# Turning the probabilities of seven head pairs on VectorE and through DRAM, in a one-core trunk layer

## The chip, the cores and the metric

The kernel runs on one core of a Trainium2 chip, in float32. The core has five engines with queues of their own: PE (TensorE, matrix products; PEld is its loading of the stationary operand), DVE (VectorE), ACT (ScalarE), POOL (GpSimd) and SP (SyncE, which here issues most DMAs). The metric is the device time of one execution in microseconds; the median of several runs counts.

## What is computed

One layer of a diffusion backbone for 128 context tokens and 256 latent tokens, width 2048: modulation by conditioning vectors, a combined projection to queries, keys, values and a Fourier group, attention, gates, an output projection, and a gated feed-forward part.

```python
sh1, sc1, g1, sh2, sc2, g2 = modulation(cond, w_mod_l, b_mod_l)
h = rms_norm(x, n1) * (1 + sc1) + sh1
q, k, v, u = project_in(h, w_in_l, qg_l, kg_l)
attn = attend(q, k, v)
x = x + g1 * token_mixing(h, attn, u, w_na_proj_l, w_fnet_proj_l, w_gate_l, w_o_l)
h2 = rms_norm(x, n2) * (1 + sc2) + sh2
x = x + g2 * swiglu(h2, w_gu_l, w_down_l)
```

Attention has 16 heads of 64. A context token attends to the 128 context tokens; a latent token to a window of the 256 latent tokens (a table of biases holds -1e30 outside it) and, in the same softmax, to 128 cached keys.

## The kernel before

**Products.** Every large weight comes in units of 256 rows by 512 columns (`load_unit`, issued on SP, four buffers). ACT makes a rounded high part `wh`, DVE the rest `wl` (`split`, L155 and L156), three buffers each; `unit` (L170, L171, L176) forms three products a block, 18 of 128x128 by 128x512 to a unit. `next_unit` is the heart of the order: it takes the `front` jobs one step further, splits the weights of the unit after this one, steps `front` and `behind` jobs, issues the load of a unit three further on, and hands the present one to PE. `mid_unit` steps `front` a third time in the middle of a unit.

**Order by pace.** All engines run their instructions in the order in which the program writes them, and that is written by generators: `Paced(gen, rate)` adds `rate` to what is due at each tick and runs a step (up to the next `yield`) for each whole one. `least` holds steps back until that many are due.

**Stages.** Opening (modulation, input projection; to about 320 us), gate stage (64 units of the gate projection, with the Fourier and attention work between them; to about 650), mixing stage (32 units), output stage (four column chunks of eight units; the first five units and the rest of the first chunk run with the row sums stopped), feed-forward part.

**Attention** is a generator in the gate stage, stepped three times a unit. `attention_pair` treats two heads: `PAIR` names what each of its 15 ticks does. `qk` turns queries and keys on PE, `s0` and `s1` form scores of the two latent token blocks (block 0 with the context tokens) and put them into `sc` (128 x 2 x 896), `m` takes maxima on DVE, `e` exponentials on ACT, `i` inverts the sums and scales `sc` on DVE (L1026). `t0` and `t1` (`keys_first`) transpose the 8 and 6 blocks of 128x128 on PE (L1039) into PSUM, from where ACT copies them (L1041) to `pt`; `pv` (`values`, L1056) multiplies by the values. `t1` and `pv` of a pair run in the next pair's ticks. `lq`, `lb`, `lv` issue the next loads.

**Row sums.** Four rows of the modulation (types 2, 4, 3, 5, in this order) are not formed on PE. `row_weights` loads 128x1024 blocks, and `mod_rows` adds them up on DVE (L361, L363; 32 such instructions for each half row, one a step). Then a chain of DMAs on POOL sums over the 128 partitions by halving (`s_sum`, L367 and L373) and adds the bias (L379, L380). `columns` reads a row back (`colr`, L391), has PE transpose it (L398) and DVE use it; type 4's columns come within type 3's sums, type 3's within type 5's, after the tenth of them. `RATES` gives the pace of these steps: at first, in the gate, mixing and output stages, and in the feed-forward part. In the output stage `rows_until` runs on until a row is done if it is not by then.

Of the kernel before, what the change touches and what calls it, by code (L numbers as in the profile page):

```python
# [13 lines left out]
F32 = mybir.dt.float32  # L14
F32R = mybir.dt.float32r
AF = mybir.ActivationFunctionType
# [3 lines left out]
P = 128  # L20
# [7 lines left out]
CTX = 128  # L28
LAT = 256
TOK = CTX + LAT  # L30
# [10 lines left out]
ORDER = [6, 7, 0, 1, 2, 3, 4, 5]  # L41
DUE = [-1.4, 0, 0, 0]
PREP = [1.75, 2.5, 1.8, 1.8]
PAIR = "t1 qk,,,,,lq,s0 s1 m0,e0,m1,i0 pv lb,e1,,i1 t0,,lv"

CHUNKS = [1.95, 1.95, 1.95, 1.6, 1.6, 1.2, 1.2, 1.7]
RATES = [1.5, 0.62, 1.1, 1.3, 0.452]
FF_PARTS = [8, 8, 8, 8, 12]  # L50


# [67 lines left out]
def trunk_kernel(ctx: ExitStack, tc: tile.TileContext, io: dict):  # L120
    nc = tc.nc
# [21 lines left out]
    dram = ctx.enter_context(tc.tile_pool(name="dram", bufs=1, space=DRAM))  # L143
# [6 lines left out]
    def nm(s):  # L150
        return f"{s}{next(ids)}"
# [133 lines left out]

    s_sum = dram.tile([P, 4 * CH], F32, tag="sum", name="s_sum")
    s_turn = dram.tile([P, 4, TOK], F32, tag="turn", name="s_turn")

    first = consts.tile([P, 96], F32, tag="first", name="first")
    conds, ng, bcol = (first[:, 32 * i : 32 * i + 32] for i in range(3))  # L290
# [16 lines left out]
    with ExitStack() as ph:  # L307
# [79 lines left out]
        def columns(ty):  # L387

            r = rpool.tile([32, P], F32, tag="colr", name=nm("colr"))
            for cnd in range(2):  # L390
                nc.gpsimd.dma_start(  # L391
                    r[16 * cnd : 16 * cnd + 16], s_row[ty][cnd].rearrange("o (k p) -> (o k) p", p=P)
                )
            yield
            yield
            yield
            o = rows_psum["tile"]()
            nc.tensor.transpose(o[:, 0:32], r, ident[:32, :32])  # L398
            ov = o[:, 0:32].rearrange("p (c k) -> p k c", c=2)
            yield  # L400
            if ty == 3:
                nc.vector.tensor_copy(msh[1], ov)
                return
            nc.vector.scalar_tensor_tensor(
                out=msc[1], in0=ov, scalar=1.0, in1=ng[:, 1].unsqueeze(2).to_broadcast([P, KT, 2]),
                op0=ALU.add, op1=ALU.mult,
            )
# [59 lines left out]
        with ExitStack() as pha:  # L467
# [37 lines left out]
            r1 = small.tile([P, NT], F32, tag="r1", bufs=1, name="r1")  # L505
# [50 lines left out]
            for t in range(NT):  # L556
                for cc in range(4):
                    turn(t, cc, acc_tile)
                    square(t, cc)
                    if t == 0 and cc == 2:  # L560
                        nc.scalar.activation(
                            out=csz[:, :, 0:2], in_=conds.rearrange("p (k c) -> p k c", c=2), func=AF.Silu
# [119 lines left out]
            for b, (i, t) in enumerate((i, t) for i in range(8) for t in range(NT)):  # L682
                ts = [slice(n * P, (n + 1) * P) for n in range(NT)]
                _, wH, wL = opened[i // 2]
                w, l = wH[:, i % 2], wL[:, i % 2]
                if b == 0:
                    po = [mm_tile() for _ in ts]
# [78 lines left out]
            for gi, (k0, n) in list(enumerate(GROUPS))[1:]:  # L766
# [5 lines left out]
                for rate, ci in zip(CHUNKS, ORDER):  # L772
                    if gi == len(GROUPS) - 1:
                        rows.rate = rate
                    po = [(mm_tile if gi < len(GROUPS) - 1 else acc_tile)() for _ in range(NT)]
# [130 lines left out]
        def attention():  # L906
            br = ph.enter_context(tc.tile_pool(name="branch", bufs=1))
            for i in range(8):
                aT[i] = br.tile([P, TOK], F32, tag=f"aT{i}", name=f"aT{i}")
            with ExitStack() as st:  # L910
                wk = st.enter_context(tc.tile_pool(name="awk", bufs=1))
                rest = {}
                for hp in range(8):
                    rest = yield from attention_pair(hp, wk, rest)
                rest["t1"]()
                for _ in range(5):
                    yield
                rest["pv"]()

        qks, vs, biases = [], [], []  # L920
        ending = [False]
# [10 lines left out]

        def load_v(hp):
            ci, co = hp // 4, (hp % 4) * P
            vp = ald.tile([P, 4, P], F32, tag="vp", bufs=2, name=nm("vp"))
            nc.sync.dma_start(vp[:, 0:3], s_qkvu[4 + ci][:, :, co : co + P])
            nc.sync.dma_start(vp[:, 3], cache_v[:, hp * P : (hp + 1) * P])
            return vp
# [7 lines left out]
        def attention_pair(hp, wk, rest):  # L946
            (_, (qp, kp)), (_, bp), (_, vp) = qks[0].take(), biases[0].take(), vs[0].take()
            t = {}

            sc = wk.tile([P, 2, 896], F32, tag="sc", name=nm("sc"))  # L950
# [70 lines left out]
            def inverses(qt):  # L1021
                sm = t["sm", qt]
                n = len(halves[qt])
                nc.vector.reciprocal(sm[:, :n], sm[:, :n])
                for i, (j, sl) in enumerate(halves[qt]):
                    nc.vector.tensor_scalar_mul(sc[:, j, sl], sc[:, j, sl], sm[:, i : i + 1])  # L1026

            def keys_first(qt):

                if not qt:  # L1030
                    t["pt"] = wk.tile([P, 16, P], F32, tag="pt", name=nm("pt"))
                blocks = [(j, qt * TOK + kc * P) for kc in range(3) for j in range(2)]
                if not qt:
                    blocks += [(j, 2 * TOK) for j in range(2)]
                for b0 in range(0, len(blocks), 4):
                    some = blocks[b0 : b0 + 4]
                    o = at_tile()
                    for i, (j, c0) in enumerate(some):
                        nc.tensor.transpose(o[:, i * P : (i + 1) * P], sc[:, j, c0 : c0 + P], ident)  # L1039
                    dst = slice(8 * qt + b0, 8 * qt + b0 + len(some))  # L1040
                    nc.scalar.copy(  # L1041
                        t["pt"][:, dst], o[:, : len(some) * P].rearrange("p (b q) -> p b q", q=P)
                    )

            def values():

                pt = t["pt"]
                po = at_tile()
                for k in range(4):
                    for j in range(2):  # L1050
                        s = slice(j * HD, (j + 1) * HD)
                        out, x = po[s, :CTX], pt[:, 6 + j]
                        if k:
                            out = po[s, CTX:TOK].rearrange("p (t q) -> p t q", t=2)
                            x = pt.rearrange("p (t b) q -> p t b q", t=2)[:, :, 2 * k - 2 + j]
                        nc.tensor.matmul(  # L1056
                            out, vp[:, k, s], x, start=k < 2, stop=k in (0, 3),
                            tile_position=(0, j * HD), skip_group_check=True,
                        )
                nc.scalar.copy(aT[hp], po[:, :TOK])  # L1060
# [2 lines left out]
                "qk": turned,  # L1063
                **{n: lambda of=of: of[0].more() for n, of in (("lq", qks), ("lb", biases), ("lv", vs))},
                **{f"{n}{j}": functools.partial(f, j) for j in range(2) for n, f in (
                    ("s", scores), ("m", maxima), ("e", exps), ("i", inverses), ("t", keys_first))},

                **{n: rest.get(n, lambda: None) for n in ("t1", "pv")},
            }
            for tick in PAIR.split(","):  # L1070
                for _ in range(3 if ending[0] and "e" in tick else 0):
# [2 lines left out]
                    work[w]()  # L1074
                soft.append("e" in tick)
                yield
            return {"t1": functools.partial(keys_first, 1), "pv": values}

        pha = ph.enter_context(ExitStack())
        ald = pha.enter_context(tc.tile_pool(name="ald", bufs=1, side="right"))  # L1080
# [9 lines left out]
        for fc8 in range(8):  # L1090
            po = [mm_tile() for _ in range(NT)]
# [76 lines left out]
        for f4 in range(4):  # L1168
            gl = [None, None]
            for i, bH, bL in ((1, fH, fL), (0, aH, aL)):  # L1170
                _, gl[i] = gates.take()
                po = [acc_tile() for _ in range(NT)]
# [82 lines left out]
    for cc in range(4):  # L1255
# [3 lines left out]
        po = [acc_tile() for _ in range(NT)] if cc else out_po  # L1259
# [365 lines left out]
```

## Time and profile before

| | us |
|---|---|
| median of 3 runs | 2005.99 |
| lowest, highest | 2004.99, 2006.89 |
| the profiled execution | 2005.29 |
| its span, first to last instruction | 2003.5 |
| PE, DVE, ACT busy in the span | 1989.5, 1226.0, 718.3 |

A row of a view of groups reads: line, engine, operation, written tile <- read tiles, shape, count, then busy time and mean ns of one, then the idle time of the engine before them and what ended it. A row of an order in time begins with start and length. Matmuls overlap, so the length of one (0.39 us for 512 columns) is more than the distance from one to the next (0.227 us); the view of the chain of work, which cuts each instruction where the next begins, gives the distance. A row of waits reads: who waited, at which line, for whom; total, times, longest.

### The profile page before, as it was taken

The numbers are of one execution on the slowest core, as the hardware profiler recorded it, in microseconds if no ns is written. First come the engines' busy times: TensorE is split into PE (matmuls) and PEld (weight loads), VectorE is DVE, ScalarE is ACT, GpSimd is POOL, SyncE is SP. The second block draws the span as 40 slices with busy tenths as digits, with TensorE's granted clock in tenths as the row PEclk, the third lists the DMA queues.
The fourth block names the chain that finished last, engine by engine and source line by source line (L and its number), as shares of the span: only waits on it lengthen the run. The fifth ranks groups of instructions, "written<-read, shape, count | busy, mean of one in ns | idle before, by whom it ended". The sixth has DMA issues, their size and how long they took to land.

```text
span 2003.5 us, 24190 instructions
## 1 busy us (share of the span) xinstructions
PE 1989.5 (99%) x9404; PEld 1628.4 (81%) x9404; DVE 1226.0 (61%) x1493; ACT 718.3 (36%) x1052; POOL 73.9 (4%) x106
## 2 busy tenths in 40 slices
PE   8999999999999999999999999999999999999999
PEld 5767888887777888889988888888888888888887
DVE  6745999879877886776843454554334433434654
ACT  6324332445554443344423322323232233223231
POOL 0000010101010100100001000001000000000000
PEclk9999999999999999999999999999999999999999
DMA  9896898888886898764457464547444544455463
GB/s 347 289 342 206 308 288 312 271 278 283 269 255 216 284 330 264 252 231 131 134 182 200 158 189 164 188 139 211 137 150 129 165 153 131 132 152 174 158 185 104
DMA packets 140658, 425.28 MB, mean 212 GB/s; under 512 B 17856, under 2 KB 39296, under 8 KB 139520
## 3 DMA queue, kind: packets, MB, share of 16 engines
q1 hardware_dynamic: 127344, 400.51, 60.4%
q0 software_dynamic: 9600, 16.88, 3.9%
q10 hardware_dynamic: 3600, 6.34, 0.9%
q8 instruction: 74, 1.21, 0.2%
q14 instruction: 40, 0.33, 0.0%
HBM read 387.50 MB, written 44.63 MB: 216 GB/s over the span
## 4 chain that ended last, share of the span: by engine, by line
PE 95%; DMA 2%; DVE 2%; ACT 1%; issue 1%; SPq 0%; DVEq 0%; ACTq 0%
PE mm L170 19%; PE mm L176 18%; PE mm L171 18%; PE at L170 10%; PE at L171 10%; PE at L176 10%; PE at L436 1%; DMA wm<-in_w_mod 1%; PE at L1039 1%; PE at L977 1%; PE at L1056 1%; DVE wl L156 1%; PE at L1447 1%; PE at L1453 1%; PE mm L1453 1%; PE mm L1447 1%
## 5 line engine op out<-in xcount | busy, mean ns | idle before, releaser
L156 DVE TENSOR_TENSOR wl<-wraw,wh 128x1024 fp32r<-128x1024 f32 (+1 forms) x464 | 553.7, 1202 | 435.1 <-ACT wh L155 251.7
L155 ACT CAST wh<-wraw 128x1024 fp32r<-128x1024 f32 (+1 forms) x464 | 478.5, 1038 | 757.9 <-PE mm L171 454.1
L170 PE MATMUL mm<-wh,hH 128*128 128x512 f32 x1316 | 518.2, 394 | 0.3 <-ACT hH L155 0.3
L171 PE MATMUL mm<-wh,hL 128*128 128x512 f32 x1316 | 513.2, 390 | 0.2
L176 PE MATMUL mm<-wl,hH 128*128 128x512 f32 x1316 | 357.2, 389 | 0.2 <-DVE wl L156 0.2
L363 DVE SCALAR_TENSOR_TENSOR accr<-wmr,csz,accr 128x1024 f32<-128x1024 f32 x240 | 301.6, 1278 | 4.6 <-DMA wmr<-in_w_rows 4.6
L170 PEld LDWEIGHTS mm<-wh,hH 128*128 128x128 f32 x1316 | 247.0, 188 | 65.6 <-issue 12.7
L176 PEld LDWEIGHTS mm<-wl,hH 128*128 128x128 f32 x1316 | 246.9, 188 | 52.2 <-DVE wl L156 0.6
L171 PEld LDWEIGHTS mm<-wh,hL 128*128 128x128 f32 x1316 | 247.2, 188 | 50.6 <-DVE hL L156 0.8
L170 PE MATMUL at<-wh,hH 128*128 128x512 f32 x616 | 240.1, 390 | 0.0
L171 PE MATMUL at<-wh,hL 128*128 128x512 f32 x616 | 239.7, 389 | 0.0
L176 PE MATMUL at<-wl,hH 128*128 128x512 f32 x616 | 169.4, 389 | 0.0
L176 PEld LDWEIGHTS at<-wl,hH 128*128 128x128 f32 x616 | 115.6, 188 | 24.0
L171 PEld LDWEIGHTS at<-wh,hL 128*128 128x128 f32 x616 | 115.7, 188 | 23.9
L170 PEld LDWEIGHTS at<-wh,hH 128*128 128x128 f32 x616 | 115.6, 188 | 23.9
L170 PE MATMUL mm<-wh,cH 128*128 128x512 f32 x278 | 108.1, 389 | 0.0
L171 PE MATMUL mm<-wh,cL 128*128 128x512 f32 x278 | 108.1, 389 | 0.0
L176 PE MATMUL mm<-wl,cH 128*128 128x512 f32 x278 | 76.6, 389 | 0.0
L170 PE MATMUL at<-wh,cH 128*128 128x512 f32 x196 | 76.2, 389 | 0.0
L171 PE MATMUL at<-wh,cL 128*128 128x512 f32 x196 | 76.2, 389 | 0.0
L783 DVE TENSOR_TENSOR acc<-acc,mm 128x512 f32<-128x512 f32 x60 | 40.4, 685 | 43.8 <-PE mm L176 43.8
L171 PEld LDWEIGHTS mm<-wh,cL 128*128 128x128 f32 x278 | 52.2, 188 | 10.8
(287 smaller groups left out, 1817.1 us busy)
## 6 DMA issues: line engine op xcount, KB each, us to landing
wraw<-in_w_gate_up SPq DMA_DIRECT2D x176, 512.0 KB, 3.8
wmr<-in_w_rows SPq DMA_DIRECT2D x128, 512.0 KB, 5.2
wraw<-in_w_down SPq DMA_DIRECT2D x88, 512.0 KB, 3.9
wraw<-in_w_gate SPq DMA_DIRECT2D x64, 512.0 KB, 5.0
wraw<-in_w_in SPq DMA_DIRECT2D x60, 512.0 KB, 5.6
wm<-in_w_mod SPq DMA_DIRECT2D x24, 768.0 KB, 6.1
wraw<-in_w_o SPq DMA_DIRECT2D x32, 512.0 KB, 6.2
wm<-in_w_mod SPq DMA_DIRECT2D x28, 512.0 KB, 6.1
```

The lines of the kernel that those rows point to most:

```text
L155: nc.scalar.copy(H, x)
L156: nc.vector.tensor_sub(L, x, fr(H))
L170: nc.tensor.matmul(po[t], H[k0 + i][:, sl], wH[:, i], start=first and i == 0, stop=False)
L171: nc.tensor.matmul(po[t], L[k0 + i][:, sl], wH[:, i], start=False, stop=False)
L176: nc.tensor.matmul(po[t], H[k0 + i][:, sl], wL[:, i], start=False, stop=last and i == n - 1)
L363: nc.vector.scalar_tensor_tensor(out=acc[:, cnd], in0=wm, scalar=sc, in1=acc[:, cnd], op0=ALU.mult, op1=ALU.add)
L436: nc.tensor.matmul(pm[q : q + 32, :w], csz[:, k, :], wm[:, kk + par, ty, :], start=k < 2, stop=k >= KT - 2, tile_position=(0, q), skip_gro ...
L783: nc.vector.tensor_add(a, a, po[t])
L977: nc.tensor.matmul(po[j][:, cols], t["q"][rows[j], q], t["k"][rows[j], k], start=True, stop=True, tile_position=(j * HD, 0),)
L1039: nc.tensor.transpose(o[:, i * P : (i + 1) * P], sc[:, j, c0 : c0 + P], ident)
L1447: nc.tensor.matmul(o, a, xH, start=u + kk == 0, stop=False)
L1453: nc.tensor.matmul(o, a, wide(u + kk)[0], start=False, stop=last and kk == 1)
```

## The change

For pairs 0 to 6 the probabilities are no longer transposed on PE. DVE transposes 32x32 blocks (`block_rows`, ticks `x0` and `x1`) into a tile `tr`, `leave` (`w0`, `w1`) writes it to DRAM, and `enter` (`r0`, `r1`, four DMAs each) reads it back so that the 32x32 blocks come to stand as a whole transpose; `pt` is now 128 x 4 x 14 x 32 and is read in runs of 32. All these DMAs are on SP. The last pair keeps `keys_first`. The product by the values runs one whole pair later, and `vp` and `pt` have one buffer more. For all pairs the scaling moves from DVE to ACT (`normed`), apart from the inversion (`inverses`). The row sums get other rates, and `columns` six `yield`s before its transpose in place of three.

```diff
-PAIR = "t1 qk,,,,,lq,s0 s1 m0,e0,m1,i0 pv lb,e1,,i1 t0,,lv"
+PAIR = "x1 qk,w1,,,r0,lq,s0 s1 m0 r1,e0,m1,v0 lb,n0 e1,v1 pv,n1 x0,w0,lv"
-RATES = [1.5, 0.62, 1.1, 1.3, 0.452]
+RATES = [1.5, 0.54, 1.16, 1.65, 0.452]
+    s_pt = [dram.tile([P, 4, n * 32], F32, tag=f"pt{n}", name=f"s_pt{n}") for n in (8, 6)]
...
-            yield
-            yield
-            yield
+            for _ in range(6):
+                yield
...
-                rest["t1"]()
-                for _ in range(5):
+                rest["x1"]()
+                for _ in range(2):
                     yield
                 rest["pv"]()
+                for _ in range(3):
+                    yield
+                rest["last"]()
...
-            vp = ald.tile([P, 4, P], F32, tag="vp", bufs=2, name=nm("vp"))
+            vp = ald.tile([P, 4, P], F32, tag="vp", bufs=3, name=nm("vp"))
...
+            def normed(qt):
+                sm = t["sm", qt]
                 for i, (j, sl) in enumerate(halves[qt]):
-                    nc.vector.tensor_scalar_mul(sc[:, j, sl], sc[:, j, sl], sm[:, i : i + 1])
+                    nc.scalar.activation(out=sc[:, j, sl], in_=sc[:, j, sl], func=AF.Copy, scale=sm[:, i : i + 1])
+            def block_rows(qt):
+                n = 6 if qt else 8
+                tr = t["tr", qt] = wk.tile([P, 4 * 8 * 32], F32, tag="tr", bufs=2, name=nm("ptr"))
+                b = tr[:, : 4 * n * 32].rearrange("p (g b r) -> p b g r", g=4, b=n)
+                for j in range(2):
+                    nc.vector.transpose(
+                        b[:, j:6:2],
+                        sc[:, j, qt * TOK : (qt + 1) * TOK].rearrange("p (c g r) -> p c g r", c=3, g=4),
+                    )
+                if not qt:
+                    nc.vector.transpose(b[:, 6:8], sc[:, :, 2 * TOK :].rearrange("p j (g r) -> p j g r", g=4))
+            def leave(qt):
+                n = 6 if qt else 8
+                nc.sync.dma_start(s_pt[qt], t["tr", qt][:, : 4 * n * 32].rearrange("p (g n) -> p g n", g=4))
+            def new_pt():
+                t["pt"] = wk.tile([P, 4, 14, 32], F32, tag="pt", bufs=2, name=nm("pt"))
+            def enter(qt):
+                if not qt:
+                    new_pt()
+                dst = t["pt"][:, :, 8:] if qt else t["pt"][:, :, :8]
+                for g in range(4):
+                    nc.sync.dma_start(
+                        dst[32 * g : 32 * g + 32].rearrange("p a b r -> p a (b r)"),
+                        s_pt[qt][:, g].rearrange("(a p) n -> p a n", p=32),
+                    )
...
-                        out, x = po[s, :CTX], pt[:, 6 + j]
+                        out, x = po[s, :CTX].rearrange("p (a r) -> p a r", a=4), pt[:, :, 6 + j]
                         if k:
-                            out = po[s, CTX:TOK].rearrange("p (t q) -> p t q", t=2)
-                            x = pt.rearrange("p (t b) q -> p t b q", t=2)[:, :, 2 * k - 2 + j]
+                            out = po[s, CTX:TOK].rearrange("p (t a r) -> p t a r", t=2, a=4)
+                            x = pt[:, :, 2 * k - 2 + j :: 8].rearrange("p a t r -> p t a r")
...
+            own = {"pv": rest.get("last", lambda: None), "last": values}
+            if hp == 7:
+                return {"x1": functools.partial(keys_first, 1), **own}
+            return {
+                "x1": functools.partial(block_rows, 1), "w1": functools.partial(leave, 1),
+                "r0": functools.partial(enter, 0), "r1": functools.partial(enter, 1), **own,
+            }
```

More of the change, by code (lines that the diff above doesn't have):

```diff
@@ L1024, in inverses @@
                 nc.vector.reciprocal(sm[:, :n], sm[:, :n])
+            def normed(qt):
+                sm = t["sm", qt]
                 for i, (j, sl) in enumerate(halves[qt]):
-                    nc.vector.tensor_scalar_mul(sc[:, j, sl], sc[:, j, sl], sm[:, i : i + 1])
+                    nc.scalar.activation(out=sc[:, j, sl], in_=sc[:, j, sl], func=AF.Copy, scale=sm[:, i : i + 1])
[24 more added lines that the diff above has]
+                    )
             def keys_first(qt):
                 if not qt:
-                    t["pt"] = wk.tile([P, 16, P], F32, tag="pt", name=nm("pt"))
+                    new_pt()
                 blocks = [(j, qt * TOK + kc * P) for kc in range(3) for j in range(2)]
@@ L1041, in keys_first @@
                     nc.scalar.copy(
-                        t["pt"][:, dst], o[:, : len(some) * P].rearrange("p (b q) -> p b q", q=P)
+                        t["pt"][:, :, dst].rearrange("p a b r -> p b a r"),
+                        o[:, : len(some) * P].rearrange("p (b a r) -> p b a r", a=4, r=32),
                     )
@@ L1065, in attention_pair @@
                 **{f"{n}{j}": functools.partial(f, j) for j in range(2) for n, f in (
-                    ("s", scores), ("m", maxima), ("e", exps), ("i", inverses), ("t", keys_first))},
-                **{n: rest.get(n, lambda: None) for n in ("t1", "pv")},
+                    ("s", scores), ("m", maxima), ("e", exps), ("v", inverses), ("n", normed))},
+                "x0": functools.partial(keys_first if hp == 7 else block_rows, 0),
+                "w0": functools.partial(leave, 0) if hp < 7 else lambda: None,
+                **{n: rest.get(n, lambda: None) for n in ("x1", "w1", "r0", "r1", "pv")},
             }
@@ L1076, in attention_pair @@
                 yield
-            return {"t1": functools.partial(keys_first, 1), "pv": values}
+            own = {"pv": rest.get("last", lambda: None), "last": values}
[5 more added lines that the diff above has]
+            }
         pha = ph.enter_context(ExitStack())
```

## The prediction

> **What bounds the kernel.** I read the page's busy times first, then what PE waited for, then the stretches.
>
> ```profile
> PE 1989.5 (99%) x9404; PEld 1628.4 (81%) x9404; DVE 1226.0 (61%) x1493; ACT 718.3 (36%) x1052; POOL 73.9 (4%) x106
> ...
> PE at L511 <- DMA xc<-in_x_in: 3.8, 1, 3.8
> PE at L436 <- DMA wm<-in_w_mod: 3.1, 5, 0.7
> PE at L1039 <- DVE sc L1026: 1.3, 2, 0.8
> ...
> 200.00:385.00 185.00, 184.81 (x846) 154.52 (x845) 168.90 (x190) 60.91 (x76) 13.89 (x18) 1.00 0.91 303
> 463.00:650.00 187.00, 186.60 (x963) 146.52 (x964) 150.25 (x196) 94.61 (x209) 17.80 (x25) 1.00 0.80 255
> 814.00:848.00 34.00, 34.00 (x157) 28.14 (x156) 27.45 (x34) 12.77 (x22) 4.84 (x7) 1.00 0.74 246
> ```
>
> The second block lists PE's waits (total, times, longest); the third gives, for a stretch, busy time of PE, PEld, DVE, ACT and POOL, the clock, the DMA share and GB/s. PE has no gap worth naming after the opening. So two things alone move the end: work taken off PE, and a wait that PE did not have. DVE at 80% and ACT at 51% in the attention stretch (463 to 650) have room.
>
> **What leaves PE.** The chain of work gives the pace of each kind (start, length, what):
>
> ```profile
> 436.00 1.22 PE at L1039 x8
> 463.40 1.22 PE at L1039 x8
> ...
> 488.39 1.66 PE at L1056 x16
> ...
> 494.36 0.87 PE at L1039 x8
> 497.97 1.36 PE mm L176 x6
> 499.34 0.66 PE at L1039 x6
> ```
>
> A transpose costs PE 0.87/8 = 0.109 us. Seven pairs lose 14 each: 98 x 0.109 = **10.7 us**. In the first two pairs the eight took 1.22 in place of 0.87, behind the waits of 1.3 us in all for the scaled rows; that goes with them, 2 x 0.35 + 1.3 = **2.0 us**. Together 12.7. Pair 7 keeps its transposes; they now wait for ACT's scaling instead of DVE's. Before, pairs 2 to 7 waited for nothing here, so I take 0 and at most the 0.8 of the worst wait above.
>
> **What moves to DVE and ACT** (of 385 to 660 by form, all eight pairs; of all the run for L1421):
>
> ```profile
> L1026 DVE TENSOR_SCALAR sc<-sc,sm 128x384 f32<-128x384 f32 x32 | 12.0, 417 | 0.6
> L1026 DVE TENSOR_SCALAR sc<-sc,sm 128x128 f32<-128x128 f32 x16 | 3.8, 283 | 0.0
> L1016 ACT ACTIVATE sc<-sc,mx 128x384 f32<-128x384 f32 x32 | 19.4, 610 | 2.9 <-DVE mx L1004 2.9
> L1016 ACT ACTIVATE sc<-sc,mx 128x128 f32<-128x128 f32 x16 | 6.2, 387 | 0.0
> L1041 ACT COPY pt<-at 128x512 f32<-128x512 f32 x24 | 13.3, 588 | 27.5 <-PE at L1039 27.5
> L1041 ACT COPY pt<-at 128x256 f32<-128x256 f32 x8 | 3.0, 378 | 0.0
> ...
> L1421 DVE STREAM_TRANSPOSE tr<-sg x30: 711/711/715, 1049.8 to 1901.1; 128x512 f32<-128x512 f32 x30
> ```
>
> DVE loses 4 x 0.417 + 2 x 0.283 = 2.2 us a pair and gets 1792 columns of block transposes in five instructions: 1792/512 x 0.711 = 2.5 by size alone, 3.6 if each cost the full 0.711. I take 2.9: +0.7. ACT gets six scalings, 4 x 0.610 + 2 x 0.387 = 3.2 at most, and loses 3 x 0.588 + 0.378 = 2.1: +1.1. Both lie beside PE's 27 us of a pair; the slower row sums take 15.4 steps (below) of 1.28 us, 20 us, off DVE in this stage, more than the 7 x 0.7 that it gains. I charge 0; if ACT held the scaled rows up by its whole 1.1, PE's margin on `wl` would absorb it, as it did the 2.9 above.
>
> `pv` a pair later changes no count of PE's instructions; at the end `pv` and `last` fall into the same five ticks in which `pv` fell. `vp` and `pt` have one buffer more for it.
>
> **The values' product** now reads runs of 32 numbers out of `pt`. No row shows PE reading such runs. The nearest: ACT's cast of `hH<-gl` reads them and `aH<-aT` doesn't, at the same size.
>
> ```profile
> L155 ACT CAST hH<-gl x12: 506/508/516, 703.9 to 771.2; 128x384 fp32r<-128x384 f32 x12
> L155 ACT CAST aH<-aT x8: 503/508/515, 653.6 to 662.2; 128x384 fp32r<-128x384 f32 x8
> ```
>
> Equal, so I take 0; a gain is excluded (same columns, same products), and the other end is half speed, 8 x 1.66 = 13.3.
>
> **The trip through DRAM.** Each pair writes and reads 4 + 3 KB for 128 partitions: 1.8 MB, in 10 DMAs on SP, 12.8 MB and 70 DMAs in all. Over 190 us that is 67 GB/s more; 15.4 steps fewer are 7.7 loads of 0.5 MB, 21 less. 255 + 46 = 301 GB/s is what 200 to 385 carried (303) with PE fed. On SP a `leave` waits for DVE's turning, an `enter` for its landing and for `values` two pairs back; behind them stand weight loads, `wmr` and the next pair's loads. Loads are queued three units (of about 5 us) before use, and these land in:
>
> ```profile
> wraw<-in_w_gate SPq DMA_DIRECT2D x47, 512.0 KB, 4.7
> ```
>
> So SP may fall back to DVE's own place in the program and 15 - 4.7 - 2.3 (cast and subtraction) leaves some 8 us. I take 0; if that cover failed, about 1 us a pair, 7 us.
>
> **The row sums' pace is the term that I weigh most.** `rows` runs one step per tick: three ticks a unit in the gate stage (64 units), one in the mixing stage (32), none for eight units, then 22 units at the fourth rate. Old against new: 192 x (0.62 - 0.54) = 15.4 steps lost, 32 x 0.06 = 1.9 won, and 3 more yields in the first `columns`: 16.4 steps behind at the end of mixing. What hangs on it is the chain of DMAs that adds up the third row over partitions, turns it, and feeds PE's transpose at L398. In order of time, before:
>
> ```profile
> L363 DVE SCALAR_TENSOR_TENSOR accr<-wmr,csz,accr x4: 1275/1278/1281, 759.1 to 772.0; 128x1024 f32<-128x1024 f32 x4
> ...
> 773.62 0.57 POOL L367 DMA_DIRECT2D s_sum<-accr  x1 [82.10 <-DVE accr L363]
> ...
> 827.75 0.78 POOL L380 DMA_DIRECT2D s_row<-s_sum  x1 [5.42 <-DMA s_row<-in_b_mod]
> 828.26 0.78 POOL L391 DMA_DIRECT2D colr<-s_row  x1
> 833.28 0.52 POOL L391 DMA_DIRECT2D colr<-s_row  x1 [4.24 <-DMA s_row<-s_sum]
> ...
> DMA to landing us min/median/max: 5.3/5.4/5.5
> ...
> L398 PE MATMUL at<-ident,colr x1: 246/246/246, 852.4 to 852.4; 32*128 32x32 f32 x1
> ...
> 1046.39 0.56 POOL L367 DMA_DIRECT2D s_sum<-accr  x1 [212.59 <-DVE accr L363]
> ...
> 1092.35 0.77 POOL L380 DMA_DIRECT2D s_row<-s_sum  x1 [3.31 <-DMA s_row<-in_b_mod]
> ```
>
> From the last sum's start (772.0) to the column's landing (833.3 + 5.4 = 838.7) 66.7 us passed; PE read it at 852.4, 14 us later. The later chain took 46.0 from first to last of these DMAs, the earlier 54.1.
>
> With the new rates: a unit is 18 products of 1.36/6 = 0.227 us, 4.08. At 772.0 some 2.3 units of mixing were left, 2.6 steps at 1.1; so the new kernel ends mixing 16.4 - 2.6 = 13.8 steps short of that sum. They come at 1.65 a unit in the second column chunk of the output stage: the last one in its eighth unit. (Counted tick by tick; with the old rates the same count puts both of PE's reads at L398 in the units where the trace has them.) From there 19 steps lead to L398: 3 for the end of the row, 10 sums, 6 yields; 19/1.65 = 11.5, so the twelfth unit. Where that is shows in DVE's order of time, where each chunk closes with L1275:
>
> ```profile
> 811.62 0.69 DVE L1275 TENSOR_TENSOR d<-at,gb 128x512 f32<-128x512 f32 x1 [4.16 <-PE at L176]
> ...
> 842.80 1.28 DVE L363 SCALAR_TENSOR_TENSOR accr<-wmr,csz,accr 128x1024 f32<-128x1024 f32 x1
> 845.71 0.69 DVE L1275 TENSOR_TENSOR d<-mm,gb 128x512 f32<-128x512 f32 x1 [1.63 <-PE mm L176]
> ```
>
> Chunks are 845.7 - 811.6 = 34.1 us. In the old kernel's time the eighth unit's first step stands at 842.8, and the second, the one in question, at about 844.5. Twelve units of 34.1/8 = 4.26 are 51 us: PE is at L398 at about 895. The chain needs 1.6 + 46 to 54 + 9 to 11 = 57 to 67 from 844.5; I take 47, since this stretch moves 246 GB/s or less and is nearer the later chain, and 10: landing at 903. **PE waits 8.4 us** there, 5 to 17 by the bounds. Steps off by a unit move it by 4.
>
> **A clock that drops.** PE's first twelve transposes, after idle time, and the windows after its last product (it ends at 1999.6) show what such a wait does:
>
> ```profile
> 3.82 2.79 PE L511 MATMUL at<-ident,xc 128*128 128x128 f32 x12 [3.82 <-DMA xc<-in_x_in]
> ...
> 2000.50:2002.00 1.50, 0.00 (x0) 0.00 (x0) 0.00 (x1) 0.00 (x0) 0.00 (x0) 1.00 0.25 87
> 2002.00:2003.50 1.50, 0.00 (x0) 0.00 (x0) 0.00 (x0) 0.00 (x0) 0.00 (x0) 0.52 0.00 0
> ```
>
> 0.232 us each in place of 0.109, and a granted clock of 0.52 from some 2.4 us after the last product. About 5 us at half pace after the wait lose **2.5 us** (0 if the clock holds, 2.8 by the rows).
>
> The Trainium skill (TensorE: Matmul & The Clock Gate, Part 1: The HAM clock gate) speaks against this change here: after an idle window of about 3.4 us the clock falls to half and takes as long a busy window to come back. By its figure the loss would be 1.7 us as an estimate, not 2.5; the trace agrees that the drop comes within about 3 us of idleness.
>
> The rates of later stages: DVE gets 0.35 x 1.28 = 0.45 us a unit more in the output stage, where it was busy 27.45 of 34 us; cost 0. The eleven sums more that are then left over come at 0.452 a unit, in 25 of the feed-forward part's 264 units, whose last row is needed in its last part.
>
> **The sum**, against the profiled run's own 2005.3 (span 2003.5): 2005.3 - 12.7 + 8.4 + 2.5 = 2003.5. The median of the runs shown, 2006.0, lies 0.7 above that run, so I say **2004.2**. Its own range, with wait and clock at their bounds, is 1998 to 2010 less the few cases of two bad ends.
>
> **Rivals.** (1) *No wait at L398*: the chain is in time, because DMAs are quicker or the steps come earlier than I count. For it: POOL has nothing else to do. Against it: it would need a chain of 39 us where the two shown take 46.0 and 54.1. It gives 2006.0 - 12.7 = 1993.3. With a short wait of 3 to 6 us it is 1996 to 2001, also faster; chance of the two 0.38, of which 0.16 for no wait.
> (2) *My forecast*, a wait of 6 to 14 us that gives the gain back: 0.49.
> (3) *The product at L1056 at half speed* on runs of 32: 2004.2 + 13.3 = 2017.5, slower. It decides from about 0.75 us more a pair (a product of 2.4 in place of 1.66), given the wait. Against it: ACT's equal casts. 0.06.
> (4) *A wait at L398 of 15 us or more*, as the slow chain of 54 us with a unit of bad luck: 2011 to 2014, 0.07.
> (5) *The change doesn't take PE's work away*: it would show as more than 14 transposes at L1039's place; nothing supports it, since the list of ticks names the block form for pairs 0 to 6.
>
> Within 0.2% (4 us, about what a measurement of this kernel tells from no change) is 2002 to 2010. The range takes in the case without a wait and stops short of (3) and (4).
>
> **What would show it.** Right: transposes at `keys_first` fall from 112 to 14, 13 us less PE work; PE's list of waits gets a line at the transpose of `colr` with 5 to 17 us in one wait, around 885 of the new span; the last sum of the third row stands about 60 us later than now, near 832. Wrong: that line is missing (then about 1993), the product's 16 take more than 1.7, or new waits for `wl` appear between 410 and 640 (SP or ACT too late).

## The result, and the profile after

| | before | after |
|---|---|---|
| median, us | 2005.49 (2004.80 to 2006.89, 4 runs) | 2029.44 (2028.00 to 2034.53, 4 runs) |
| the profiled execution and its span | 2005.29, 2003.5 | 2034.53, 2032.8 |

The ratio is 1.0122 (1.0105 to 1.0139): the change makes the kernel slower by 24 us. The forecast missed: it was 2004.2, from 1998 to 2010 with wait and clock at their bounds, and 1993 if the wait at L398 stayed away. The profiled execution of after is the longest of its four, some 5 us over the median.

Busy times of after, from the page:

```profile
PE 1989.2 (98%) x9306; PEld 1622.5 (80%) x9306; DVE 1226.2 (60%) x1480; ACT 725.5 (36%) x1072; POOL 73.5 (4%) x106
```

98 matmuls are gone, as the change says (9404 before), and the others are the same; the span is 29 us longer. So the time is in PE's waits and in its pace. The waits of PE after, of the whole run (who, at which line, for whom; total, times, longest):

```profile
PE at L398 <- DMA colr<-s_row: 13.2, 1, 13.2
PE mm L176 <- DVE wl L156: 7.1, 4, 3.2
PE at L1076 <- ACT sc L1032: 4.8, 2, 4.6
...
PE mm L170 <- ACT wh L155: 2.1, 3, 1.0
PE at L170 <- ACT wh L155: 2.1, 1, 2.1
```

The first line is the forecast's. The others, 16 us, are new: of these four, before's list had only the second, at 0.2 us (the 1.3 us that it had at the old transposes, L1039, are gone). Where they are, the stretches show (PE, PEld, DVE, ACT, POOL, clock, DMA share, GB/s); after:

```profile
430.00:640.00 210.00, 195.25 (x925) 148.33 (x924) 157.28 (x201) 113.34 (x264) 18.56 (x26) 0.98 0.97 304
...
900.00:930.00 30.00, 16.78 (x67) 13.54 (x67) 9.30 (x12) 7.54 (x11) 5.95 (x9) 0.77 0.39 116
```

and before:

```profile
430.00:640.00 210.00, 208.67 (x1073) 163.50 (x1073) 171.35 (x229) 112.10 (x252) 18.58 (x26) 1.00 0.82 261
...
900.00:930.00 30.00, 30.00 (x157) 27.06 (x156) 19.29 (x32) 11.74 (x25) 0.00 (x0) 1.00 0.47 153
```

There are two main places: attention in the gate stage, where PE stood idle for 15 us while the DMA share rose from 0.82 to 0.97, and the single wait at the transpose of `colr`. The last line of the list, 2.1 us, lies apart from both, in the mixing stage (it ends at 751.9). A further loss is seen in short windows laid over the records of the granted clock (stretches of after):

```profile
499.90:503.30 3.40, 3.40 (x10) 2.64 (x9) 3.40 (x6) 3.40 (x6) 0.00 (x0) 0.51 1.05 398
636.50:639.90 3.40, 3.40 (x13) 2.91 (x12) 0.76 (x2) 3.40 (x9) 0.52 (x1) 0.50 1.02 352
752.50:755.90 3.40, 3.40 (x10) 2.63 (x9) 3.40 (x4) 2.73 (x4) 0.78 (x1) 0.50 1.02 411
...
921.50:926.60 5.10, 5.10 (x16) 4.26 (x17) 1.50 (x5) 3.79 (x7) 0.00 (x0) 0.50 0.00 0
```

PE worked at half clock three times for 3.4 us, and for 5.1 us after the long wait: 3 x 1.7 + 2.55 = 7.7 us lost. Before had no such window until its end. Together, for the two profiled executions: 12.7 less work, 13.2 + 16.1 of waits, 7.7 of clock: +24.3 of the 29.3 by which the spans differ. Of the other 5 us, 1.7 are small waits further down the same list (`wm` 3.7 for 3.1, `gst` 1.1 for none). The list leaves hardly any idle time out: PE's, span less busy time, grew from 14.0 to 43.6 us, and the waits listed grew from 9.5 to 39.0. So the last 3 us lie in time that counts as busy; where, is not shown.

How the weights come late can be read around 497 us. First SP's issues after the change, in order of time (start, length):

```profile
473.93 0.33 SPq L230 DMA_DIRECT2D wraw<-in_w_gate  x1
479.00 3.77 SPq L1060 DMA_DIRECT2D pt<-s_pt  x4
485.30 0.53 SPq L931 DMA_DIRECT2D qp<-s_qkvu  x1
...
487.92 1.73 SPq L1060 DMA_DIRECT2D pt<-s_pt  x4
489.75 0.38 SPq L230 DMA_DIRECT2D wraw<-in_w_gate  x1
490.18 0.42 SPq L341 DMA_DIRECT2D wmr<-in_w_rows  x1
```

then DVE's:

```profile
485.82 1.26 DVE L364 SCALAR_TENSOR_TENSOR accr<-wmr,csz,accr 128x1024 f32<-128x1024 f32 x1
497.04 1.28 DVE L364 SCALAR_TENSOR_TENSOR accr<-wmr,csz,accr 128x1024 f32<-128x1024 f32 x1 [9.96 <-DMA wmr<-in_w_rows]
...
498.31 1.21 DVE L156 TENSOR_TENSOR wl<-wraw,wh 128x1024 fp32r<-128x1024 f32 x1
```

and PE's:

```profile
499.57 2.64 PE L176 MATMUL mm<-wl,hH 128*128 128x512 f32 x6 [3.25 <-DVE wl L156]
```

For 16 us SP issued no weights: eight transfers of the way in and a pair's loads stood between. Its records show eight semaphores taken in turn, so each issue waits until the transfer eight places before it has landed. `wmr`, issued at 490.2, landed at 497.0; DVE waited 10 us for it, and `wl`, which DVE forms behind it, came 3.25 us late for PE. The waits on the queues from 385 to 660 us tell the same in sums. After, SP's, ACT's and DVE's:

```profile
SPq L1060 <- DMA wraw<-in_w_gate: 11.7, 7, 2.4
SPq L1060 <- DMA wmr<-in_w_rows: 11.1, 7, 4.7
...
ACT wh L155 <- DMA wraw<-in_w_gate: 23.9, 9, 8.3
...
DVE accr L364 <- DMA wmr<-in_w_rows: 23.3, 7, 10.0
```

Before, SP waited for buffers to come free, that is, it was ahead, and neither ACT nor DVE waited for a load:

```profile
SPq L230 <- DVE wl L156: 85.7, 31, 9.0
SPq L340 <- DVE accr L363: 64.2, 27, 7.9
```

After, these two are 61.2 and 6.8: SP is still ahead part of the time with the weights, but hardly with the row loads. Landing times in the attention stretch (median, us) were 4.9 for `wraw` and 4.7 for `wmr` before, and 6.9 for `wmr` after; `wraw` before, then after:

```profile
wraw<-in_w_gate SPq DMA_DIRECT2D x37, 512.0 KB, 4.9
...
wraw<-in_w_gate SPq DMA_DIRECT2D x37, 512.0 KB, 7.5
```

What was costed at nothing on the engines is nothing. After, by form:

```profile
L1040 DVE STREAM_TRANSPOSE ptr<-sc 128x384 f32<-128x384 f32 x28 | 14.4, 554 | 0.0
L1094 PE MATMUL at<-pt,vp 128*64 128x256 f32 x96 | 11.7, 379 | 0.0
...
L1045 DVE STREAM_TRANSPOSE ptr<-sc 128x256 f32<-128x256 f32 x7 | 2.8, 405 | 0.0
```

The block transposes take 4 x 0.554 + 0.405 = 2.6 us a pair (2.9 taken), and the product by the values takes 379 ns on runs of 32, as it did before (x96, 11.7 us, 379).

### The profile page after: what moved, and what is told of

Same layout as the page of the kernel before. It is cut to its first block, busy times and chain, and to the rows that moved or that the text cites. A ratio compares the mean times of both kernels' runs of the same rounds, so it can differ in the third digit from the quotient of the medians.

```text
span 2032.8 us, 24108 instructions
## 1 busy us (share of the span) xinstructions
PE 1989.2 (98%) x9306; PEld 1622.5 (80%) x9306; DVE 1226.2 (60%) x1480; ACT 725.5 (36%) x1072; POOL 73.5 (4%) x106
## 4 chain that ended last, share of the span: by engine, by line
PE 83%; DMA 7%; DVE 5%; ACT 2%; issue 2%; SPq 0%; ACTq 0%; POOL 0%; DVEq 0%; POOLq 0%
PE mm L170 16%; PE mm L171 16%; PE mm L176 16%; PE at L170 10%; PE at L171 10%; PE at L176 10%; DMA s_sum<-s_sum 2%; DMA wmr<-in_w_rows 2%; DVE wl L156 1%; DVE accr L364 1%; PE at L436 1%; DMA wm<-in_w_mod 1%; DMA s_sum<-accr 1%; ACT wh L155 1%; PE at L1492 1%
## 5 line engine op out<-in xcount | busy, mean ns | idle before, releaser
L170 PE MATMUL mm<-wh,hH 128*128 128x512 f32 x1316 | 520.7, 396 | 3.5 <-ACT wh L155 2.1
L170 PEld LDWEIGHTS mm<-wh,hH 128*128 128x128 f32 x1316 | 248.5, 189 | 72.5 <-issue 13.1
L170 PE MATMUL at<-wh,hH 128*128 128x512 f32 x616 | 240.0, 390 | 0.0
L170 PEld LDWEIGHTS at<-wh,hH 128*128 128x128 f32 x616 | 115.7, 188 | 24.0
L170 PE MATMUL mm<-wh,cH 128*128 128x512 f32 x278 | 108.1, 389 | 0.0
L170 PE MATMUL at<-wh,cH 128*128 128x512 f32 x196 | 76.2, 389 | 0.0
L170 PEld LDWEIGHTS mm<-wh,cH 128*128 128x128 f32 x278 | 52.2, 188 | 10.8
```

Source lines behind the costliest of these rows:

```text
L170: nc.tensor.matmul(po[t], H[k0 + i][:, sl], wH[:, i], start=first and i == 0, stop=False)
```

## The experiments

Theory: two causes that add up, the pace of the row sums (a wait at L398) and the trip through DRAM (weights late through SP). Rivals: the scaling on ACT; the trip's bytes rather than its place in SP's order. All were timed in three rounds beside before.

| run | from | median, us | ratio to before |
|---|---|---|---|
| e1_rows_only | before, new row pace | 2021.88 | 1.0072 (1.0057 to 1.0087) |
| e2_trip_only | after, old row pace | 2026.82 | 1.0098 (1.0082 to 1.0113) |
| e3_scale_only | before, scaling on ACT | 2008.29 | 1.0007 (0.9997 to 1.0016) |
| e4_no_trip | after, no trip | 2012.31 | 1.0030 (1.0017 to 1.0042) |
| e5_act_queue | after, trip issued by ACT | 2056.23 | 1.0252 (1.0237 to 1.0267) |
| e6_slots | e4, ten tiny transfers a pair | 2013.85 | 1.0038 (1.0024 to 1.0052) |
| e7_bytes | e4, the trip's bytes in four | 2018.61 | 1.0063 (1.0048 to 1.0078) |
| e8_no_trip_paced | e4, an earlier row pace | 2000.26 | 0.9968 (0.9958 to 0.9979) |
| e9_trip_paced | after, that row pace | 2022.05 | 1.0076 (1.0052 to 1.0101) |
| e10_five | after, five transfers a pair | 2027.79 | 1.0093 (1.0065 to 1.0121) |
| e11_direct | e9, sixteen inside SBUF | 2033.79 | 1.0144 (1.0126 to 1.0163) |
| e12_pool_queue | e9, trip issued by POOL | 2040.85 | 1.0172 (1.0157 to 1.0187) |
| e13_five_paced | e10, that row pace | 2014.00 | 1.0044 (1.0027 to 1.0061) |
| e14_five_spread | e13, the way in spread out | 2019.35 | 1.0064 (1.0049 to 1.0079) |
| e15_five_late | e14, three steps later | 2021.85 | 1.0086 (1.0059 to 1.0113) |

### The parts alone

**e1_rows_only**, before with:

```diff
-RATES = [1.5, 0.62, 1.1, 1.3, 0.452]
+RATES = [1.5, 0.54, 1.16, 1.65, 0.452]
...
-            yield
-            yield
-            yield
+            for _ in range(6):
+                yield
```

> The kernel before with the changed pace of the row sums alone (the five rates, six yields in columns). Theory: the slowdown has two separate causes, the wait for the turned row at the transpose of colr (13.2 us in the changed kernel's profile, then some 5 us at half clock) and the crowding of SP and the DMA engines in the gate stage by the trip through DRAM. Then this kernel has the first and not the second: 2005.5 + 13 + 3 = 2021, from 2014 to 2025, one wait of 8 to 16 us at L398 and none over 1 us in the gate stage. Rival: the row sums alone cost all of it, 2029 or more. Second rival: the wait at L398 only arises because the crowded DMAs lengthen the chain; then no wait over 3 us there and 2005 to 2009.

Measured 2021.88, 16 us more than before. The first of its waits of PE:

```profile
PE at L397 <- DMA colr<-s_row: 14.0, 1, 14.0
```

The new pace alone makes the wait (L397 is that transpose in this kernel) and nothing in the gate stage. It also makes the small wait in the mixing stage: 1.9 us for `wh` at L170, at 739.9; e4, without the trip, has 1.1 there, and before and e2, with the old pace, have none.

**e2_trip_only**, after with the old `RATES` and three `yield`s:

> The changed kernel with the old rates and three yields in columns. Theory: no wait at the transpose of colr in the output stage, but the gate stage is as crowded as in the changed kernel or more, since 15 more row sum steps and their loads fall into it: 2005.5 - 12.7 + 15 to 30 us of waits and half-clock windows = 2008 to 2023, DMA share 0.95 or more from 430 to 640. Rival (the row sums' pace causes nearly all): 1993 to 1998.

2026.82. PE waited 6.8 us for `wh` and 5.5 for `wl` in the gate stage, and PE was busy for 188.21 of the 210 us there. A wait of 8.3 us for the first columns (type 4's, read in the gate stage) came on top, since the chain ran longer beside the trip (59.6 us from its first transfer to its last into `s_row`, 52.5 before) and three steps no longer covered it; this I had not counted, and the time is above what I gave.

**e3_scale_only**, before with the scaling on ACT (`normed` in place of the product in `inverses`):

> The kernel before with only the scaling of the probabilities moved from VectorE to ScalarE (ticks v and n, as in the changed kernel); transposes stay on PE. Theory: a later scaling costs PE little, 2004 to 2009, PE's waits at keys_first under 3 us in all. Rival (the scaling on ScalarE, behind the casts of the weights, is what holds PE's weights up in the changed kernel): 2012 or more, with waits for wl or sc in the gate stage of 7 us or more.

2008.29, not told apart from before; 2.2 us of waits for the scaled rows in all. The scaling isn't the cause.

**e4_no_trip**. The block transposes write straight into `pt`, and the 70 transfers are left out, so that in pairs 0 to 6 the 32x32 blocks don't stand where the product by the values needs them:

```diff
-                tr = t["tr", qt] = wk.tile([P, 4 * 8 * 32], F32, tag="tr", bufs=2, name=nm("ptr"))
-                b = tr[:, : 4 * n * 32].rearrange("p (g b r) -> p b g r", g=4, b=n)
...
+                b = (t["pt"][:, :, 8:] if qt else t["pt"][:, :, :8]).rearrange("p g b r -> p b g r")
```

> The changed kernel without the 70 DMAs through DRAM: VectorE's blocks are written straight into the tile that the product reads (three buffers), so the blocks of pairs 0 to 6 stand at the wrong places and the attention output of these heads differs. All else, the new rates too, as changed. Theory (the trip crowds SP and the DMA engines): the gate stage's waits go, the wait at L398 stays: 2005.5 - 12.7 + 16 = 2009, from 2004 to 2013; DMA share from 430 to 640 back to about 0.8. Rival (VectorE's transposes or ScalarE's scaling hold the weights up): 2022 or more, with waits for wl as before.

2012.31: 17.1 us less than after. Its attention stretch:

```profile
430.00:640.00 210.00, 210.00 (x1038) 162.82 (x1037) 161.24 (x205) 121.80 (x276) 18.57 (x26) 1.00 0.79 257
```

PE is never idle there, the clock holds, and the wait for `colr` (13.4 us) is left, and no wait for pair 7's scaled rows: that one of after, 4.8 us, was the trip's doing as well.

### What of the trip

**e5_act_queue**, `leave` and `enter` with `nc.scalar.dma_start`:

> The changed kernel, rates included, with the 70 DMAs of the trip issued on ScalarE's queue in place of SP's. In the profile of the changed kernel SP's DMAs take eight semaphores in turn, and each waits until the one eight before it has landed; the eight small reads of a pair use up a whole turn. Theory S (SP's turn of eight in flight is what makes weights and row loads late): waits for wl, wh and wmr in the gate stage mostly go, the wait at the transpose of colr stays: 2029 - 15 = 2014, from 2009 to 2019. Theory B (bytes and packets crowd the DMA engines themselves, share 0.97): 2025 to 2033, with the share still at 0.95 or more.

2056.23, neither of the two. The largest of ACT's waits from 385 to 660 us shows why:

```profile
ACT wh L155 <- DMA pt<-s_pt: 36.0, 5, 9.4
```

ACT issues in order too: standing before a transfer, it doesn't cast. `wraw` landed in 5.0 us and still `wh` was late. Only the place of the blockage moved.

**e6_slots** is e4 with ten transfers of 32 bytes a partition for each pair, at the trip's places on SP; **e7_bytes** is e4 with all the trip's bytes a pair, out and in, as four transfers that each reach all 128 partitions, the way in with rows of 4 and 3 KB into a tile that nobody reads. In both the blocks stay as in e4.

> As the run without the trip (blocks written straight into the product's tile, wrong places for pairs 0 to 6), plus the ten DMAs of each pair in their ticks on SP, but of 32 bytes a partition and with the reads going to a tile that nobody uses: places in SP's queue and its turn of eight, hardly any bytes. Theory S: gate stage waits of 7 us or more for wl, wh or wmr come back, 2012 + 8 to 15 = 2020 to 2027. Theory B: 2008 to 2015, DMA share from 430 to 640 about 0.8.

> As the run without the trip, plus its bytes in four DMAs a pair in place of ten (the two writes as in the change, each read in one piece of 128 partitions to a tile that nobody uses, rows of 4 or 3 KB): bytes with few places in SP's queue. Theory S: 2008 to 2016. Theory B: 2020 to 2030, DMA share 0.9 or more and weight loads landing in 6 us or more.

2013.85 and 2018.61, so 1.5 and 6.3 us over e4, where the trip costs 17.1: e6 as theory B has it, e7 between the two theories. e7's attention stretch has the higher traffic of the two kernels and yet little idle time:

```profile
430.00:640.00 210.00, 205.96 (x1011) 158.73 (x1009) 160.93 (x204) 118.38 (x271) 18.57 (x26) 0.99 0.93 314
```

314 GB/s against 304 of after: the bandwidth is there. The packets on SP's queue in this stretch are as many, too, 30183 against 30232 (20904 in e4). Neither the turns alone nor the bytes and packets alone make the 17 us.

**e8_no_trip_paced** and **e9_trip_paced** are e4 and after with

```diff
-RATES = [1.5, 0.54, 1.16, 1.65, 0.452]
+RATES = [1.5, 0.54, 1.6, 1.4, 0.452]
...
-            for _ in range(6):
+            for _ in range(9):
```

so that the sums come earlier and the read later (e8's blocks are as e4's).

> The run without the trip, with another pace: rates 0.54, 1.6, 1.4 and nine yields, so that by my count of steps the last sum of the third row stands in the second unit of the second column chunk and PE's read at the transpose of colr some 15 units later, 60 us. Theory: no wait there over 2 us, none elsewhere: what the transposes are worth to PE, 2005.5 - 12.7 = 1993, from 1991 to 1997. Rival (something else in the change costs time too): above 1999.

> The kernel after the change with the row steps of run e8_no_trip_paced: nine steps before the read of the columns, and rates 1.6 and 1.4 in the mixing and output stages. If the two causes are independent (the row pace gives the 13.4 us wait at the transpose of colr, the trip through DRAM gives the weight waits in the gate stage), the time falls by what the same edit took from the kernel without the trip, 2012.3 to 2000.3, so 12 us: 2017.4 (2014 to 2021), with no wait over 1 us for colr, the gate-stage waits for wl and wh still at 9 to 15 us in sum, and two to five small waits in the mixing stage of some 6 us together. Rival: the two cover each other, because slower rows relieve the gate stage and the late weights delay the rows; then under half of the 12 us comes back: 2023 to 2028. If the time is under 2012, the trip itself costs less than the 17 us that I give it.

2000.26 and 2022.05. The wait for `colr` is gone in both. In e8, 12 us came back, and 5.6 us of small waits stay, most in the mixing stage, where DVE is now busy for 96.6 of 110 us; so the time lies above the 1991 to 1997 written down. In e9 only 7.4 came back: its waits of PE are

```profile
PE mm L176 <- DVE wl L156: 8.0, 4, 3.2
...
PE at L176 <- DVE wl L156: 3.4, 1, 3.4
PE at L1076 <- ACT sc L1032: 3.0, 1, 3.0
PE mm L170 <- ACT wh L155: 2.6, 3, 1.1
```

with four windows at half clock, 3.4 to 6.8 us each. So the causes nearly add up, but not wholly; at this pace the trip costs 2022.05 - 2000.26 = 21.8 us.

**e10_five**: one `leave` and four `enter`s for a pair, at the places of the second half's; the same bytes, half the packets, and one buffer of block rows in place of two.

```diff
+            def leave(qt):
+                if qt:
+                    nc.sync.dma_start(s_pt, t["tr"].rearrange("p g b r -> p g (b r)"))
...
+                for g in range(4):
+                    nc.sync.dma_start(
+                        t["pt"][32 * g : 32 * g + 32].rearrange("p a b r -> p a (b r)"),
+                        s_pt[:, g].rearrange("(a p) n -> p a n", p=32),
+                    )
```

> The kernel after the change with one transfer out and four in for a pair (at the places of the second half's), in place of two and eight: the same bytes, through the same DRAM, with rows of 1.8 KB in place of 1.0 and 0.75 KB, so half the transfers and half the packets. If it is the number of transfers in SP's order together with the bytes that makes the weights late, the time lies between that of the same bytes in four transfers (2018.6) and after (2029.4): 2019 to 2024; the waits of PE for wl and wh between 430 and 640 us fall under 8 us in sum, and DVE's wait for wmr at the row sums under 23 us. Rival: the bytes and the dependence of the way in on the way out do it, whatever the number: 2026 to 2031, with the waits as after the change. Under 2017 the packets were the cause, not the transfers.

Its executions spread from 2018.98 to 2029.92, median 2027.79: inconclusive by time. PE's waits for `wl` and `wh` fell to 5.9 us (11.3 in after), as expected, but 15.0 us at `colr` (13.2 in after) took part of it back: a kernel that comes sooner to a chain that runs at its own pace waits longer for it.

**e13_five_paced** is the same at e9's row pace, where that can't happen:

> Run e10_five (one transfer out and four in for a pair) with the row steps of e9_trip_paced (nine steps before the read, rates 1.6 and 1.4), so that a wait at the transpose of colr can't take back what the gate stage gains. If the number of transfers in SP's order is the cause, halving it takes about half of the 22 us that the trip costs at this pace (2022.05 less 2000.3): 2009 to 2015, and the waits for wl and wh in the gate stage are under 7 us. Rival: what counts is the burst, four transfers of 7 us behind one another, which is as it was: 2017 to 2023.

2014.00, as expected: 8 us of the trip's 21.8 are gone with half the transfers, and half their packets, at equal bytes; that the packets alone don't set the time, e7 shows.

**e11_direct** (sixteen transfers a pair inside SBUF, no DRAM, half the bytes) and **e12_pool_queue** (e9 with `nc.gpsimd.dma_start` for the trip):

```diff
+                for g in (2 * qt, 2 * qt + 1):
+                    for a in range(4):
+                        nc.sync.dma_start(
+                            t["pt"][32 * g : 32 * g + 32, a], t["tr"][32 * a : 32 * a + 32, g]
+                        )
```

> The kernel of run e9_trip_paced without the trip through DRAM, but with the blocks still moved by transfers: one buffer of block rows for a pair, and sixteen transfers of 57 KB from partition block to partition block inside SBUF, eight at each of the two places of the way in. So half the bytes of the trip (0.92 in place of 1.84 MB a pair), no way in that waits for a way out, but sixteen turns in SP's order in place of ten. If bytes and turns only hurt together, as the runs with the one or the other alone say (1.5 us for ten small transfers, 6.3 us for all the bytes in four), it is 2000.3 of run e8_no_trip_paced and 2 to 8 us: 2002 to 2008, with under 5 us of waits for wl and wh in the gate stage, and wraw landing in about 6 us. Rival: the number of transfers in SP's order is what counts once each of them is of a size that lands in microseconds; then sixteen are worse than ten: 2022 or more, with SP waiting for transfers of its own ahead of wraw and wmr.

> The kernel of run e9_trip_paced with both ways of the trip issued by POOL in place of SP: the same bytes and transfers, off SP's order; POOL has only the sums over rows in the gate stage. If SP's order is what makes the weights late, the waits for wl and wh in the gate stage fall under 5 us in sum and the time comes to that of run e8_no_trip_paced and the price of the bytes alone, 2000.3 and 6: 2006 (2002 to 2011). Rival: the traffic itself makes them late, on whatever queue: 2018 to 2026, with wraw landing in 7 us and waits as in e9_trip_paced. If POOL is held by the way in as ACT was, it is DVE's row sums that wait for POOL to fetch them, and the time is over 2026.

e11 took 2033.79, 12 us more than e9, with a DMA share of 0.84 in place of 0.98 in the attention stretch. SP's, then ACT's and DVE's waits:

```profile
SPq L1058 <- DMA wraw<-in_w_gate: 15.8, 11, 2.8
...
ACT wh L155 <- DMA wraw<-in_w_gate: 19.8, 5, 5.8
...
DVE ptr L1040 <- DMA pt<-ptr: 14.9, 5, 4.7
```

Half the bytes, fewer packets (25273 on SP's queue there, 30193 in e9) and a worse time: it doesn't go by the bytes. The run isn't quite clean, since it had one buffer of block rows and DVE waited 14.9 us for it. e12 took 2040.85, near the third case written down, though it was DVE's blocks and not its row sums that waited for POOL. ACT's and DVE's waits in its attention:

```profile
ACT wh L155 <- DMA wraw<-in_w_gate: 3.9, 2, 3.4
...
DVE ptr L1040 <- DMA s_pt<-ptr: 37.3, 2, 20.6
```

Off SP's order, ACT's wait for `wraw` fell from 24.1 (e9) to 3.9 us, DVE's for `wmr` from 22.1 to none in the list, and SP was ahead again (115 us of waits for a buffer of `wl`'s). In their place POOL, held by its chain of sums, read `ptr` so late that DVE stood 37 us before its next blocks and PE 14.5 + 18.6 behind it. That SP was ahead isn't only because PE stood still: from 530 to 605 us, with 23 of the trip's transfers issued, a DMA share of 1.04 to 1.06 and `wraw` landing in 7.5 us as in after, PE was busy for 74.99 of 75 us. So SP's order is what held the weights; each other queue holds its own engine's work. The Trainium skill (DMA: Bandwidth & Descriptors, Issuing engines are not separate DMA queues) says that DMAs of all engines share 16 DMA engines and that spreading them saves only issue time. Traffic did stay in the way (`wraw` landed in 6.3 us), but what the queue decided here was which engine stood behind a transfer's wait.

**e14_five_spread** and **e15_five_late** issue e13's four ways in at four ticks of a pair; e15 begins at e13's tick, e14 three sooner:

```diff
-PAIR = "x1 qk,w1,,,r0,lq,s0 s1 m0 r1,e0,m1 r2,v0 lb,n0 e1 r3,v1 pv,n1 x0,w0,lv"
+PAIR = "x1 qk,w1,,,,lq,s0 s1 m0 r0,e0,m1 r1,v0 lb,n0 e1 r2,v1 pv,n1 x0 r3,w0,lv"
```

> The same as e13_five_paced, with the four transfers in issued at four places of a pair, two steps or more apart, in place of all at one. If a burst of transfers holds SP's turn and with it the weights behind, this takes most of what is left: 2002 to 2008, no wait for wl or wh over 1.5 us in the gate stage. If it is only the number of turns, it comes out as e13_five_paced within 3 us.

> Run e14_five_spread with its first way in three steps later, at the place where e13_five_paced issues all four, and the others two steps apart behind it. In e14_five_spread SP stood 41.7 us of the gate stage waiting for the way out to land before the first way in, against 13.7 in e13_five_paced, and the time was 5.3 us longer. If that wait on SP is what made it worse, it falls to 15 us or less here, and the time is that of e13_five_paced or, if the burst costs something of its own, less: 2007 to 2015. If spreading the four is itself harmful (each of them late among the weights), it stays at 2017 to 2021 with SP's wait for the way out gone.

2019.35 and 2021.85, both slower than e13 in medians, with intervals that just overlap its own. In e14 SP stood 41.7 us before the first way in until the way out had landed; in e15 that is 13.5 us, as in e13 (13.7), and the time isn't better. So nothing speaks for the burst as the harm; the same four come out worse between the weights than in one place. Why, the runs don't settle: `wraw` landed in 8.8 us in e15 against 7.4 in e13, and DVE waited 21.9 us for `wmr` against 14.1. No version with the trip came out ahead of before; e8, which did, leaves out the moving of the blocks.

## Why the prediction was wrong

In medians, each run against the one before it in the table:

| step | forecast | measured |
|---|---|---|
| row pace: wait and clock | 8.4 + 2.5 = +10.9 | e1 - before: 2021.88 - 2006.05 = +15.8 |
| transposes off PE | -12.7 | e4 - e1: 2012.31 - 2021.88 = -9.6 |
| trip through DRAM | 0, or 7 if the cover failed | after - e4: 2029.44 - 2012.31 = +17.1 |
| sum | -1.8 | +23.4 |

- **The step that failed is "The trip through DRAM", with its "I take 0".** It compared 301 GB/s with the 303 that an earlier stretch had carried with PE fed. The rate was forecast right, 304, and didn't decide: in e12, at a mean of 330 GB/s from 530 to 605 us, PE was fed while the trip went by another queue. The second argument, some 8 us in hand for one load that SP issues late, took the landing time of before (4.7 us), which rose to 7.5, and counted one delay, where ten transfers a pair each take a turn in SP's order and the row loads stand in that order too. The rest follows from DVE's and ACT's own order: a late `wmr` holds `wl`. The 7 us of the failing cover were also too few, 17.1 to 21.8 by the runs. The sign of failure that the prediction named, new waits for `wl` between 410 and 640, is what appeared. What of the trip fills SP's order stays open in part: tiny transfers in the same places cost 1.5 us and the bytes in four transfers 6.3, so it takes both, but no run parts the number of transfers from their reaching only 32 partitions each on the way in.
- **The wait at L398**: mechanism right, size low. The forecast was 8.4 within 5 to 17; it was 13.2, and 13.2 to 17.0 in six further kernels with that pace. The chain after:

```profile
867.26 0.57 POOL L368 DMA_DIRECT2D s_sum<-accr  x1 [88.79 <-DVE accr L364]
...
916.97 0.77 POOL L381 DMA_DIRECT2D s_row<-s_sum  x1 [1.52 <-DMA s_row<-in_b_mod]
...
L398 PE MATMUL at<-ident,colr x1: 282/282/282, 921.5 to 921.5; 32*128 32x32 f32 x1
```

It took 49.7 us from its first transfer (867.3) to its last into `s_row` (917.0), where 47 was taken, and the columns landed 4.4 us later, where 10 was taken. What was misread is the tick of the last sum: the forecast puts it in the eighth unit of the second chunk, 1.2 us ahead of the chunk's close, though its own 13.8 steps at 1.65 a unit make 8.4 units. It started at 865.7, 7.1 us behind that close (858.6). PE came to its read 49.7 us behind the close, where the forecast has 49.3. So 8.3 us of a later sum and 2.7 of a longer chain stand against 5.6 of quicker columns: that the wait stayed within its bounds is in part luck.
- **The clock**: 2.5 us taken after that wait, 2.55 measured. Three further windows of 3.4 us, 5.1 us in all, were not forecast; two follow the trip's waits, and the third, at 752.5, follows the wait in the mixing stage, which the new row pace makes without the trip (e1).
- **98 transposes**: the count is right. e4 and e1 differ by 9.6 of 12.7 us, but e4's executions spread from 2009.18 to 2015.04. The profiled executions settle it: without the waits listed for PE and the time lost at half clock, the spans differ by 10.8 us (e4 against e1) and 10.7 (e8 against before), and 98 x 0.109 is 10.7.
- **Pair 7's wait**, "at most 0.8": 4.8, through the trip; none without it in e4.
- **Block transposes, scaling, strided product at 0**: right (2.6 us a pair beside PE's work; e3; 379 ns before and after). The rival of a product at half speed is refuted.
- **The chances**: 0.13 for slower was too little, and no rival for the slow side was built on SP, though the prediction named what stands behind each `leave` and `enter`.

## What to carry to other kernels

Before a transfer is put on a queue, list what is issued behind it and how far ahead that was: a stage whose loads wait only for buffers has cover, and here it was spent by transfers that took turns ahead of the loads on the issuing queue. A mean rate that another stage has carried says little of it. And when a step is moved against a chain of DMAs that runs at its own pace, a gain ahead of the chain's reader is given back at the reader until the reader is moved too.

## What the runs showed of the hardware

- PE's clock fell to half after waits shorter than a window: a wait of 2.10 us ended at 751.93 in after, and the clock was at half from 752.5 for 3.4 us. The waits of 2.15 us in e8 and 2.13 in e14 were followed by such windows too, one of 2.88 in after (to 627.8) wasn't. The Trainium skill (TensorE: Matmul & The Clock Gate, Part 1: The HAM clock gate) gives windows of 3413 ns that run freely and a drop after an idle one; the length agrees, and the runs show that a gap of 2 us can do.
- After the 13.2 us wait PE ran 5.1 us at half clock before it had its pace back.
- The same bytes, in as many packets, at 314 GB/s in four transfers a pair cost 6.3 us (e7), at 304 GB/s in ten transfers 17.1 (after).
- Loads that land late need not hold PE: with the trip issued by POOL, `wraw` landed in 7.5 us from 530 to 605 us, as in after, and PE had no wait there (e12).
